# mLSTM heads with the bound on the squares and one f32 sum per token tile; a sixth output tile beside the last head

## The chip, the cores and the metric

The kernel runs on one core of one Trainium2 chip. The metric is the device time of one execution in microseconds (us), from three runs of the kernel before: 1195.31 us in the median, 1194.69 to 1196.02. A difference is told from no change here if it is over about 0.2%.

## The reference, cut to what matters

A trunk of two layers on 512 tokens of width 1024, all in float32. The first layer has four mLSTM heads of 192 columns beside four heads of attention to a memory; their outputs are joined to a mix of 1024 columns, multiplied by an output matrix and added to x. Then a gated MLP with a causal convolution follows; the second layer has band attention in place of the mLSTM. Of the mLSTM head, this counts here:

```python
num = einsum('bhts,bhse->bhte', s, vv) + inter[..., None] * einsum('bhtd,bhde->bhte', qq, c_st)
den = sum(s, axis=-1) + inter * einsum('bhtd,bhd->bht', qq, n_st)
h = num / maximum(abs(den), exp(-m_t))[..., None]
...
hm = hm * rsqrt(mean(hm * hm, axis=-1, keepdims=True) + EPS)      # per head, 192 columns
mix_out = hm * a_head_g * sigmoid(o)
...
x = x + concatenate([mix_out, mem_out], axis=-1) @ w_out
```

Since the division by the denominator and the norm are both factors per token, the kernel folds them into one: rsqrt(mean(num^2) + EPS * max(den^2, exp(-2 m_t))).

## The kernel before

Activations lie transposed: 128 features on the partitions, the 512 tokens (S) along the row; eight such tiles (KT) make up the width. A float32 product is made of three products of the faster fp32r type: both operands are split into a high part (cast, on ScalarE, L130) and a low part (difference, on VectorE, L131), and `mm3` (L167) issues high x high, high x low, low x high. Those three are called a triple here. A few small products stay in plain f32.

**A head (`mlstm_head`, L1144).** The whole sequence is worked as one causal square in four blocks of 128 tokens. `weighted_scores(s)` makes key-by-query scores in a "sc" bank of PSUM and weights them with spread exponents (L1155 to L1167); `products(s)` multiplies them by the values into two "tr" banks, `nums[0]` and `nums[1]`. A head has 192 columns: 128 in `nums[0]`, and 64 in one half of `nums[1]`. The value tiles carry 128 columns of ones between the heads' values, so that the other 64 rows of `nums[1]` all hold the denominator. Then come the squares of both banks on ScalarE (L1193), the product of the numerators and the output gate on VectorE (L1195), and per token tile two f32 products on TensorE (L1200, L1201) with the constant `mcf`: they give two columns per token, the sum of the numerators' squares and the denominator's square. Behind them are the maximum with `floor2` (L1205), two more small steps (L1206, L1207), an inverse square root in integer and float steps (`rsqrt`, L213), a diagonal matrix of the factor (`diagonal`, L231), its spread over the partitions by TensorE (`spread`, L244), the product with the gated numerators (L1214) and the split into the mix tiles (L1217). Heads 0 and 1 fill mix tiles 0 to 2, heads 2 and 3 tiles 3 to 5 (head 3: tile 5 and half of tile 4); the memory heads fill 6 and 7.

**The bound.** `gate_rows` (L1031) computes the gates' running sums as rows of 4 x 512 (head x token); `mr` (L1091, L1092) becomes m_t, at least -40. Four TensorE transposes (L1097) turn it into token columns, and one exponential (L1099) makes `floor2`.

**The order of the work.** Outside the blocks under `manual_schedule`, the order of the code is a wish: the framework orders each engine's instructions by its own estimate of when they are ready, with the code's order as priority; what is wrapped in `pin` keeps its place. Jobs are generators; `weave(job, filler, each)` (L200) advances the job, and for each of its yields (a bare one counts 1, `yield 2.673` counts 2.673) it takes `each` times so many steps of the filler, one step being a triple. In heads 0 to 2 the filler is the rest of the input projection (112 triples: tiles 2 to 5 and two tiles of memory queries). In the second memory attention and in head 3 it is the output projection.

**The output projection (`OutProjection`, L607).** Before, groups of output tiles accumulate early, in open banks: tiles 0 to 2 in the "mm" banks, 3 and 4 in the "tr" banks; `part(g, *ks)` loads and splits the weights of group g for the mix tiles ks and adds their products. `finish` (L627) takes the remaining output tiles (5, 6 and 7) as full projections, adds the residual (L633), and accumulates the squares of the next norm. The second layer uses the same class (L1380), with groups (0, 3) and (3, 5).

**Buffers.** Weights go through rings of three: "wr" as loaded, "wh" and "wl" the two parts. "u" has 57 tiles of 128x512, "t" eight. PSUM: three "mm" banks, three "sc", two "tr".

Of the kernel before, what the change touches and what calls it, by code (L numbers as in the profile page):

```python
# [9 lines left out]
F32 = mybir.dt.float32  # L10
# [3 lines left out]
ALU = mybir.AluOpType  # L14
# [41 lines left out]
def trunk(  # L56
# [30 lines left out]
    def sb(tag, shape, dtype=F32):  # L87
        count[0] += 1
        return pool.tile(shape, dtype, tag=tag, name=f"{tag}{count[0]}", bufs=bufs[tag])
# [23 lines left out]
    eps = cpool.tile([P, 1], F32, name="eps")  # L113
    V.memset(eps, EPS)

    mcf = cpool.tile([P, 3, 2], F32, name="mcf")
    V.memset(mcf, 0.0)
    V.memset(mcf[:, 0, 0:1], 1.0)
    V.memset(mcf[:HD, 1, 0:1], 1.0)
    V.memset(mcf[HD:, 1, 1:2], 1.0 / HD)  # L120
    V.memset(mcf[:HD, 2, 1:2], 1.0 / HD)
    V.memset(mcf[HD:, 2, 0:1], 1.0)


    HEADS = (slice(0, HD), slice(HD, P))

    pin = tc.keep_in_program_order
# [32 lines left out]
    def weights(*args):  # L160
        return parts(load(*args))

    def rows(w, c0, n, k0=0, k1=None):
        k1 = k1 if k1 is not None else w.shape[0] // P
        return w[k0 * P : k1 * P, c0 : c0 + n].rearrange("(k p) c -> p k c", p=P)
# [4 lines left out]
        nc.tensor.matmul(o, lh, rl, start=False, stop=False, skip_group_check=more)  # L170
        nc.tensor.matmul(o, ll, rh, start=False, stop=last, skip_group_check=more)  # L171

    def project(w, c0, act, tag="mm"):


        n = len(act)
        wh, wl = weights(rows(w, c0, P), n, P)
        o = ps(tag)
        for k in range(n):
            mm3(o, wh[:, k, :], wl[:, k, :], act[k][0], act[k][1], k == 0, k == n - 1)  # L180
            yield
        return o

    def run(gen):
        while True:
            try:
                next(gen)
            except StopIteration as end:
                return end.value

    def chain(*gens):
        for g in gens:
            yield from g
# [53 lines left out]
    def logarithms():  # L247

        pin(A.preload_act_table_set("natural_log_exp_and_others"))
# [357 lines left out]
    class OutProjection:  # L607
# [18 lines left out]

        def finish(self, gnames):  # L627
            logarithms()
            norm = Norm()
            acts = [[] for _ in gnames]  # L630
            for j in range(KT):
                o = self.o[j] if j in self.o else run(project(self.w, j * P, self.mixes))
                V.tensor_add(xT[j], xT[j], o)  # L633
                pin(G.dma_start(xspill[j], xT[j]))
                norm.add(xT[j])
                for a, g in zip(acts, gnames):
                    a.append(scaled(xT[j], g[:, j : j + 1]))
            return norm, acts
# [373 lines left out]
    e, u, c, r = (cpool.tile([P, TT, AH], F32, name=f"gate{i}") for i in range(4))  # L1012
    tot = cpool.tile([AH, 16], F32, name="tot")
    acol = cpool.tile([P, TT, AH], F32, name="acol")
    floor2 = cpool.tile([P, TT, AH], F32, name="floor2")
    NEXT = 4
    RO = [0, 512, 896, 1152, 1280]

# [12 lines left out]
    def gate_rows():  # L1031
# [58 lines left out]
            spread_exponents(i)  # L1090
        pin(V.tensor_tensor(out=mr, in0=mr, in1=br, op=ALU.add))  # L1091
        V.tensor_scalar(mr, mr, -40.0, None, op0=ALU.max)  # L1092
        yield
        tp = ps("tr")
        for T in range(TT):
            nc.tensor.transpose(tp[:, T * AH : (T + 1) * AH], ar[:, T * P : (T + 1) * P], ident[:AH, :AH])
            nc.tensor.transpose(tp[:, 16 + T * AH : 16 + (T + 1) * AH], mr[:, T * P : (T + 1) * P], ident[:AH, :AH])  # L1097
        pin(V.tensor_copy(acol, tp[:, :16].rearrange("p (t h) -> p t h", t=TT)))
        A.activation(floor2, tp[:, 16:32].rearrange("p (t h) -> p t h", t=TT), AF.Exp, scale=-2.0)  # L1099

    mixes = [None] * KT

# [41 lines left out]
    def mlstm_head(h):  # L1144
# [43 lines left out]
        yield from products(2)  # L1188
        yield from products(3)
        sqs = []  # L1190
        for o, j, r in ((nums[0], full, slice(0, P)), (nums[1], sh, rs)):
            sq = sb("t", [P, S])
            A.activation(sq, o, AF.Square)  # L1193
            sqs.append(sq)
            V.tensor_tensor(out=og[j][r, :], in0=o[r, :], in1=og[j][r, :], op=ALU.mult)  # L1195
        yield
        st = ps("sc")
        for T in range(TT):
            sl = slice(T * P, (T + 1) * P)
            nc.tensor.matmul(st[:, 2 * T : 2 * T + 2], sqs[0][:, sl], mcf[:, 0, :], start=True, stop=False)  # L1200
            nc.tensor.matmul(st[:, 2 * T : 2 * T + 2], sqs[1][:, sl], mcf[:, 1 + odd, :], start=False, stop=True)  # L1201
            yield 0.581
        st = st[:, : 2 * TT].rearrange("p (t c) -> p t c", c=2)
        z, fc = small(), small()
        V.tensor_tensor(out=z, in0=st[:, :, 1], in1=floor2[:, :, h], op=ALU.max)  # L1205
        V.tensor_scalar(z, z, EPS, 1e-35, op0=ALU.mult, op1=ALU.max)  # L1206
        V.scalar_tensor_tensor(z, st[:, :, 0], 1.0 / DH, z, op0=ALU.mult, op1=ALU.add)  # L1207
        rsqrt(fc, z)
        dg = diagonal(fc)
        yield 2.673  # L1210
        fb = spread(dg, "sc")
        yield
        for j, r in ((full, slice(0, P)), (sh, rs)):
# [2 lines left out]
                mixes[j] = sb("u", [P, S], F32R), sb("u", [P, S], F32R)  # L1216
            split(mixes[j][0][r, :], mixes[j][1][r, :], og[j][r, :])  # L1217

    outp = OutProjection(a_w_out, mixes, (0, 3, "mm"), (3, 5, "tr"))
    run(value_columns(1))  # L1220
    load_vectors(1)
    load_vectors(2)
# [16 lines left out]
    job = mlstm_head(3)  # L1239
    fill = chain(fill, outp.part(0, 7))  # L1240
    weave(islice(job, 13), fill, 0.85)
    fill = chain(fill, outp.part(1, 0, 1, 2, 6), outp.part(1, 3, 7))
    weave(job, fill, 0.862)
    run(chain(fill, outp.part(0, 4, 5), outp.part(1, 4, 5)))
    norm, (act,) = outp.finish([col["gffn"][:, 0:8]])


# [275 lines left out]
```

## Time and profile before

| What | Value |
|---|---|
| Median of three runs | 1195.31 us (1194.69 to 1196.02) |
| The profiled execution | 1195.72 us, span 1194.0 us |
| Granted TensorE clock | 0.999 of full speed |
| TensorE busy (PE) | 1183.5 us, 99% of the span |
| VectorE busy (DVE) | 961.7 us, 81% |
| ScalarE busy (ACT) | 725.2 us, 61% |
| GpSimd busy (POOL) | 130.3 us, 11% |
| Heads 0 to 3 with what is woven in | about 88 to 254 us of the span |

In the profile's lines, PE is TensorE's products, PEld its weight loads (beside PE), DVE VectorE, ACT ScalarE, POOL GpSimd, SP the queue that issues most DMAs. A line of a timeline gives start, length, engine, source line, operation, what it writes and reads (buffer numbers left out; psc, pmm and ptr are PSUM banks), its shape and how many like it were merged; in brackets stands the idle time before it and what ended that. The end of a TensorE product is modelled, so that lengths overlap; starts are measured.

### The profile page before, as it was taken

The page shows a single profiled execution, that of the slowest core. Times are in us where ns is not written, and L with a number is a line of the kernel's source. Part 1 is how long each engine was busy: PE and PEld are TensorE (multiplying, and loading weights), DVE is VectorE, ACT ScalarE, POOL GpSimd, SP SyncE. Part 2 cuts the span into 40 slices and gives each one's busy share as a digit, 9 for nine tenths or more (in the row PEclk, how much of TensorE's full clock was granted, in tenths as well). Part 3 has the DMA queues.
Part 4 walks back from the last instruction along what each step waited for, and adds up shares of the span by engine and source line. Part 5 has one row for each costly group of instructions (what it writes and reads, how often), then busy time and mean ns, then how long its engine had stood idle before and what let it go on. Part 6 is the DMA issues. An engine that isn't in the chain of part 4 may idle for free.

```text
span 1194.0 us, 18184 instructions
## 1 busy us (share of the span) xinstructions
PE 1183.5 (99%) x6719; PEld 1037.0 (87%) x6719; DVE 961.7 (81%) x1760; ACT 725.2 (61%) x1294; POOL 130.3 (11%) x222
## 2 busy tenths in 40 slices
PE   9999999999999999999999999999999999999997
PEld 9988888888899998999888888888889988999986
DVE  6877788788978888888698888997896888888855
ACT  5648677655656555555576677776565655555545
POOL 1211201010021111111020000101001011011100
PEclk9999999999999999999999999999999999999999
DMA  8645313444265676665464313246336455665551
GB/s 289 212 108 140 84 54 80 152 144 141 88 156 147 156 165 165 154 144 123 142 204 123 89 54 101 69 135 185 111 99 141 116 139 135 142 141 139 119 158 71
DMA packets 200155, 158.61 MB, mean 133 GB/s; under 512 B 8344, under 2 KB 179838, under 8 KB 200066
## 3 DMA queue, kind: packets, MB, share of 16 engines
q1 hardware_dynamic: 183906, 119.74, 34.1%
q0 software_dynamic: 15584, 36.67, 14.9%
q8 instruction: 53, 0.87, 0.3%
q10 hardware_dynamic: 576, 1.05, 0.2%
q14 instruction: 36, 0.29, 0.1%
HBM read 128.89 MB, written 32.46 MB: 135 GB/s over the span
## 4 chain that ended last, share of the span: by engine, by line
PE 92%; ACT 3%; DVE 2%; DMA 1%; SPq 1%; issue 0%; POOL 0%; POOLq 0%; DVEq 0%; ACTq 0%
PE pmm L169 15%; PE pmm L170 15%; PE pmm L171 15%; PE ptr L171 6%; PE ptr L169 6%; PE ptr L170 6%; PE pmm L785 6%; PE psc L171 5%; PE psc L170 5%; PE psc L169 5%; PE pmm L784 3%; PE psc L519 2%; PE ptr L1350 1%; DMA wr<-in_mem_w_kv_dram 1%; PE ptr L1371 1%; PE ptr L1372 1%
## 5 line engine op out<-in xcount | busy, mean ns | idle before, releaser
L169 PE MATMUL pmm<-u,wh 128*128 128x512 f32 (+1 forms) x872 | 309.1, 355 | 0.3 <-ACT u L130 0.2
L170 PE MATMUL pmm<-u,wh 128*128 128x512 f32 (+1 forms) x872 | 306.2, 351 | 0.0
L171 PE MATMUL pmm<-u,wl 128*128 128x512 f32 (+1 forms) x872 | 306.0, 351 | 0.0
L131 DVE TENSOR_TENSOR wl<-wr,wh 128x1024 fp32r<-128x1024 f32 (+3 forms) x172 | 199.8, 1163 | 57.0 <-ACT wh L130 55.0
L130 ACT CAST wh<-wr 128x1024 fp32r<-128x1024 f32 (+3 forms) x172 | 172.4, 1004 | 97.7 <-PE pmm L170 44.5
L171 PEld LDWEIGHTS pmm<-u,wl 128*128 128x128 f32 x872 | 164.5, 189 | 21.1
L169 PEld LDWEIGHTS pmm<-u,wh 128*128 128x128 f32 x872 | 164.5, 189 | 18.5 <-ACT u L130 1.1
L170 PEld LDWEIGHTS pmm<-u,wh 128*128 128x128 f32 x872 | 164.7, 189 | 18.2 <-DVE u L131 0.5
L169 PE MATMUL ptr<-u,wh 128*128 128x512 f32 x272 | 106.7, 392 | 0.0
L171 PE MATMUL ptr<-u,wl 128*128 128x512 f32 x272 | 106.1, 390 | 0.0
L753 POOL DMA_DIRECT2D xspill<-t x64 | 55.6, 869 | 461.1 <-ACT t L752 450.4
L170 PE MATMUL ptr<-u,wh 128*128 128x512 f32 x272 | 105.9, 389 | 0.0
L130 ACT CAST u<-pt 128x512 fp32r<-128x512 f32 x102 | 63.0, 620 | 46.8 <-DVE pt L875 46.7
L131 DVE TENSOR_TENSOR u<-pt,u 128x512 fp32r<-128x512 f32 x102 | 69.9, 688 | 11.2 <-ACT u L130 8.5
L169 PE MATMUL psc<-u,wh 128*128 128x256 f32 (+1 forms) x232 | 76.1, 328 | 0.0
L171 PE MATMUL psc<-u,wl 128*128 128x256 f32 (+1 forms) x232 | 75.9, 327 | 0.0
L170 PE MATMUL psc<-u,wh 128*128 128x256 f32 (+1 forms) x232 | 75.9, 327 | 0.0
L937 ACT ACTIVATE t<-t 128x512 f32<-128x512 f32 x34 | 21.6, 634 | 79.3 <-DVE t L660 79.3
L785 PE MATMUL pmm<-u,u 128*128 128x512 f32 x192 | 69.6, 397 | 0.0
L821 DVE TENSOR_TENSOR t<-t,pmm 128x256 f32<-128x256 f32 x72 | 30.2, 419 | 44.9 <-ACT t L819 44.8
L752 ACT COPY t<-ptr 128x512 f32<-128x512 f32 x64 | 37.4, 585 | 43.1 <-PE ptr L171 43.1
L660 DVE SCALAR_TENSOR_TENSOR t<-t,cols,t 128x511 f32<-128x511 f32 x80 | 59.7, 746 | 3.7 <-ACT t L667 3.7
(300 smaller groups left out, 2673.8 us busy)
## 6 DMA issues: line engine op xcount, KB each, us to landing
wr<-in_ffn_w_up_dram SPq DMA_DIRECT2D x54, 512.0 KB, 4.2
wr<-in_ffn_w_down_dram SPq DMA_DIRECT2D x38, 512.0 KB, 4.1
pt<-in_ffn_w_up_dram SPq DMA_DIRECT2D x34, 512.0 KB, 6.2
xspill<-t POOLq DMA_DIRECT2D x64, 256.0 KB, 5.2
wr<-in_a_w_in_dram SPq DMA_DIRECT2D x20, 512.0 KB, 3.7
xspill<-u POOLq DMA_DIRECT2D x32, 256.0 KB, 2.6
u<-xspill SPq DMA_DIRECT2D x32, 256.0 KB, 5.0
wr<-in_w_kv_dram SPq DMA_DIRECT2D x12, 512.0 KB, 3.7
```

Source lines behind the costliest of these rows:

```text
L130: high = A.copy(hi, src) if on_act else V.tensor_copy(hi, src)
L131: low = V.tensor_tensor(out=lo, in0=src, in1=f(hi), op=ALU.subtract)
L169: nc.tensor.matmul(o, lh, rh, start=first, stop=False, skip_group_check=more)
L170: nc.tensor.matmul(o, lh, rl, start=False, stop=False, skip_group_check=more)
L171: nc.tensor.matmul(o, ll, rh, start=False, stop=last, skip_group_check=more)
L519: nc.tensor.matmul(o, a, b, start=first and i == 0, stop=i == 1)
L660: V.scalar_tensor_tensor(acc[:, n:], src[:, : S - n], self.fw[:, c * FT + j : c * FT + j + 1], acc[:, n:], op0=ALU.mult, op1=ALU.add,)
L752: A.copy(t, o)
L753: G.dma_start(xspill[j], t, accum_op=ALU.add)
L784: nc.tensor.matmul(r[:, :H], w[1][:, k], p[i - 1][:, :H], start=False, stop=False, skip_group_check=True)
L785: nc.tensor.matmul(r, w[0][:, k], p[i - 1], start=False, stop=k == n - 1, skip_group_check=True)
L821: V.tensor_tensor(out=o, in0=o, in1=r[:, H:], op=ALU.add)
```

## The change

The bound is no longer turned into token columns. `mr` is made into max(EPS * 3 * exp(-2 m), 1e-35) as rows (DH / HD is 3, the factor between a sum over 64 equal rows and a mean over 192 columns), stored in DRAM, and loaded back as two "u" tiles in which the row of a head fills the 64 partitions where its denominator stands. In a head, the squares of `nums[1]` now come first; VectorE scales the denominator's half of them and takes the maximum with the bound, adds the two square tiles, and does the gate products after that. TensorE sums the added tile with a column of ones: one f32 product per token tile in place of two. After the sums one small step is left of three. The yields before the sums and before the spread change. In the output projection, tile 5 becomes a third group in a "sc" bank, its products beside the end of head 3, ahead of the group in the "tr" banks; `finish` loads and splits the weights of the first two remaining tiles before anything else, in both layers.

```diff
--- before.py
+++ after.py
@@ -113,15 +113,6 @@
     eps = cpool.tile([P, 1], F32, name="eps")
     V.memset(eps, EPS)
 
-    mcf = cpool.tile([P, 3, 2], F32, name="mcf")
-    V.memset(mcf, 0.0)
-    V.memset(mcf[:, 0, 0:1], 1.0)
-    V.memset(mcf[:HD, 1, 0:1], 1.0)
-    V.memset(mcf[HD:, 1, 1:2], 1.0 / HD)
-    V.memset(mcf[:HD, 2, 1:2], 1.0 / HD)
-    V.memset(mcf[HD:, 2, 0:1], 1.0)
-
-
     HEADS = (slice(0, HD), slice(HD, P))
 
     pin = tc.keep_in_program_order
@@ -170,11 +161,11 @@
         nc.tensor.matmul(o, lh, rl, start=False, stop=False, skip_group_check=more)
         nc.tensor.matmul(o, ll, rh, start=False, stop=last, skip_group_check=more)
 
-    def project(w, c0, act, tag="mm"):
+    def project(w, c0, act, tag="mm", ready=None):
 
 
         n = len(act)
-        wh, wl = weights(rows(w, c0, P), n, P)
+        wh, wl = ready or weights(rows(w, c0, P), n, P)
         o = ps(tag)
         for k in range(n):
             mm3(o, wh[:, k, :], wl[:, k, :], act[k][0], act[k][1], k == 0, k == n - 1)
@@ -626,10 +617,12 @@
 
         def finish(self, gnames):
             logarithms()
+            rest = [j for j in range(KT) if j not in self.o]
+            ready = {j: weights(rows(self.w, j * P, P), KT, P) for j in rest[:2]}
             norm = Norm()
             acts = [[] for _ in gnames]
             for j in range(KT):
-                o = self.o[j] if j in self.o else run(project(self.w, j * P, self.mixes))
+                o = self.o[j] if j in self.o else run(project(self.w, j * P, self.mixes, ready=ready.get(j)))
                 V.tensor_add(xT[j], xT[j], o)
                 pin(G.dma_start(xspill[j], xT[j]))
                 norm.add(xT[j])
@@ -1012,7 +1005,8 @@
     e, u, c, r = (cpool.tile([P, TT, AH], F32, name=f"gate{i}") for i in range(4))
     tot = cpool.tile([AH, 16], F32, name="tot")
     acol = cpool.tile([P, TT, AH], F32, name="acol")
-    floor2 = cpool.tile([P, TT, AH], F32, name="floor2")
+    floor2 = dram.tile([AH, S], F32, name="floor2")
+    floors = []
     NEXT = 4
     RO = [0, 512, 896, 1152, 1280]
 
@@ -1090,13 +1084,20 @@
             spread_exponents(i)
         pin(V.tensor_tensor(out=mr, in0=mr, in1=br, op=ALU.add))
         V.tensor_scalar(mr, mr, -40.0, None, op0=ALU.max)
+        A.activation(mr, mr, AF.Exp, scale=-2.0)
+        V.tensor_scalar(mr, mr, EPS * DH / HD, 1e-35, op0=ALU.mult, op1=ALU.max)
+        G.dma_start(floor2, mr)
+        for hp in range(2):
+            floors.append(sb("u", [P, S]))
+            for odd, half in enumerate(reversed(HEADS)):
+                row = floor2[2 * hp + odd]
+                src = bass.AP(tensor=row.tensor, offset=row.offset, ap=[[0, HD], [1, S]])
+                G.dma_start(floors[hp][half, :], src)
         yield
         tp = ps("tr")
         for T in range(TT):
             nc.tensor.transpose(tp[:, T * AH : (T + 1) * AH], ar[:, T * P : (T + 1) * P], ident[:AH, :AH])
-            nc.tensor.transpose(tp[:, 16 + T * AH : 16 + (T + 1) * AH], mr[:, T * P : (T + 1) * P], ident[:AH, :AH])
         pin(V.tensor_copy(acol, tp[:, :16].rearrange("p (t h) -> p t h", t=TT)))
-        A.activation(floor2, tp[:, 16:32].rearrange("p (t h) -> p t h", t=TT), AF.Exp, scale=-2.0)
 
     mixes = [None] * KT
 
@@ -1188,26 +1189,26 @@
         yield from products(2)
         yield from products(3)
         sqs = []
+        for o in reversed(nums):
+            sqs.insert(0, sb("t", [P, S]))
+            A.activation(sqs[0], o, AF.Square)
+        dr = HEADS[1 - odd]
+        V.scalar_tensor_tensor(
+            sqs[1][dr, :], sqs[1][dr, :], EPS * DH / HD, floors[hp][dr, :], op0=ALU.mult, op1=ALU.max
+        )
+        V.tensor_add(sqs[0], sqs[0], sqs[1])
         for o, j, r in ((nums[0], full, slice(0, P)), (nums[1], sh, rs)):
-            sq = sb("t", [P, S])
-            A.activation(sq, o, AF.Square)
-            sqs.append(sq)
             V.tensor_tensor(out=og[j][r, :], in0=o[r, :], in1=og[j][r, :], op=ALU.mult)
         yield
+        yield 3.6
         st = ps("sc")
         for T in range(TT):
-            sl = slice(T * P, (T + 1) * P)
-            nc.tensor.matmul(st[:, 2 * T : 2 * T + 2], sqs[0][:, sl], mcf[:, 0, :], start=True, stop=False)
-            nc.tensor.matmul(st[:, 2 * T : 2 * T + 2], sqs[1][:, sl], mcf[:, 1 + odd, :], start=False, stop=True)
-            yield 0.581
-        st = st[:, : 2 * TT].rearrange("p (t c) -> p t c", c=2)
+            nc.tensor.matmul(st[:, T : T + 1], sqs[0][:, T * P : (T + 1) * P], ones[:, :1], start=True, stop=True)
         z, fc = small(), small()
-        V.tensor_tensor(out=z, in0=st[:, :, 1], in1=floor2[:, :, h], op=ALU.max)
-        V.tensor_scalar(z, z, EPS, 1e-35, op0=ALU.mult, op1=ALU.max)
-        V.scalar_tensor_tensor(z, st[:, :, 0], 1.0 / DH, z, op0=ALU.mult, op1=ALU.add)
+        V.tensor_scalar(z, st[:, :TT], 1.0 / DH, None, op0=ALU.mult)
         rsqrt(fc, z)
         dg = diagonal(fc)
-        yield 2.673
+        yield 4.2
         fb = spread(dg, "sc")
         yield
         for j, r in ((full, slice(0, P)), (sh, rs)):
@@ -1216,7 +1217,7 @@
                 mixes[j] = sb("u", [P, S], F32R), sb("u", [P, S], F32R)
             split(mixes[j][0][r, :], mixes[j][1][r, :], og[j][r, :])
 
-    outp = OutProjection(a_w_out, mixes, (0, 3, "mm"), (3, 5, "tr"))
+    outp = OutProjection(a_w_out, mixes, (0, 3, "mm"), (3, 5, "tr"), (5, 6, "sc"))
     run(value_columns(1))
     load_vectors(1)
     load_vectors(2)
@@ -1239,9 +1240,9 @@
     job = mlstm_head(3)
     fill = chain(fill, outp.part(0, 7))
     weave(islice(job, 13), fill, 0.85)
-    fill = chain(fill, outp.part(1, 0, 1, 2, 6), outp.part(1, 3, 7))
+    fill = chain(fill, outp.part(2, 0, 1, 2, 3, 6, 7), outp.part(1, 0, 1, 2, 6), outp.part(1, 3, 7))
     weave(job, fill, 0.862)
-    run(chain(fill, outp.part(0, 4, 5), outp.part(1, 4, 5)))
+    run(chain(fill, outp.part(0, 4, 5), outp.part(1, 4, 5), outp.part(2, 4, 5)))
     norm, (act,) = outp.finish([col["gffn"][:, 0:8]])
```

## The prediction

> **What bounds the kernel now.** First the profile's page: its first section and the shares of the chain that ended last.
>
> ```profile
> PE 1183.5 (99%) x6719; PEld 1037.0 (87%) x6719; DVE 961.7 (81%) x1760; ACT 725.2 (61%) x1294; POOL 130.3 (11%) x222
> ...
> PE 92%; ACT 3%; DVE 2%; DMA 1%; SPq 1%; issue 0%; POOL 0%; POOLq 0%; DVEq 0%; ACTq 0%
> ```
>
> TensorE is busy for 99% of the span and is 92% of the chain: what shortens the run is a TensorE instruction less or a TensorE wait less, and work added on VectorE or ScalarE costs nothing until TensorE waits for it. Then the busy time of the stretch from the end of the gate rows to the end of head 3 (columns: length, then PE, PEld, DVE, ACT, POOL).
>
> ```profile
> core 0: us, PE busy (x) PEld busy (x) DVE busy (x) ACT busy (x) POOL busy (x), PEclk, DMA share, GB/s
> 88.00:254.00 166.00, 165.52 (x840) 138.89 (x839) 127.21 (x260) 114.80 (x193) 15.62 (x34) 1.00 0.39 102
> ```
>
> The stretch is like the whole: TensorE 165.52 of 166 us at full granted clock, VectorE 77%, ScalarE 69%. But a TensorE "busy" time is a modelled end; pace is read from start to start. So third, TensorE's timeline at head 3's sums.
>
> ```profile
> 241.49 0.28 PE L1200 MATMUL psc<-mcf,t 128*128 128x2 f32 x2
> 241.63 0.36 PE L1201 MATMUL psc<-mcf,t 128*128 128x2 f32 x2
> 241.85 0.36 PE L1200 MATMUL psc<-mcf,t 128*128 128x2 f32 x2
> 242.07 0.36 PE L1201 MATMUL psc<-mcf,t 128*128 128x2 f32 x2
> 242.30 0.49 PE L169 MATMUL ptr<-u,wh 128*128 128x512 f32 x1
> 242.62 0.40 PE L170 MATMUL ptr<-u,wh 128*128 128x512 f32 x1
> 242.85 0.40 PE L171 MATMUL ptr<-u,wl 128*128 128x512 f32 x1
> ```
>
> Ordinary 512-column products start 0.23 us apart (242.62 to 242.85); three of them, L169 to L171, are one triple, 0.69 us. Every f32 sum in the code stands as x2 in the trace, so one call is two passes. They have two columns each but a full 128x128 weight tile, and come about 0.11 us apart.
>
> **The change part by part.** *The f32 sums.* Eight passes and the product behind them take 242.62 − 241.49 = 1.13 us; less an ordinary 0.23 that is 0.90 us for eight passes, the slow restart of L169 (0.32) included. A head has four token tiles with two calls of two passes, 16 passes, two such blocks: 1.80 us. After the change it has four calls, eight passes: one block, 0.90. Lone calls would each pay the restart: the first two passes take 0.14 and the restart adds 0.09, 0.23 a call, 0.92 a head. A moving operand of one column instead of two changes nothing that I can see here, since the pace is far above two columns' share of 0.23. Saved: 0.9 us a head (0.88 to 0.9), 3.6 us for four heads, all of it on TensorE.
>
> The Trainium skill, page "TensorE: Matmul & The Clock Gate", section "Back-to-back issue gap", gives about 81 ns as the sustained spacing of a weight load and a small product; by it the 32 passes removed are worth 2.6 us. The 0.11 us of the rows is nearer to the weight load's own length by the same page, section "LDWEIGHTS" (columns / 1.2, so 107 ns), and I take the rows.
>
> *The transposes of the bound.* Four of L1097 go from the gate rows.
>
> ```profile
> 88.44 0.20 PE L1097 MATMUL ptr<-ident,t 4*128 4x4 f32 x1
> 88.50 0.20 PE L1096 MATMUL ptr<-ident,t 4*128 4x4 f32 x1
> ```
>
> They stand 0.06 us apart: 4 x 0.06 = 0.25 us saved.
>
> *The end of head 3.* Its rows 4 and 5 of the mix are the last thing that the output projection waits for.
>
> ```profile
> 251.75 0.39 PE L171 MATMUL ptr<-u,wl 128*128 128x512 f32 x1
> 252.30 0.96 PE L169 MATMUL pmm<-u,wh 128*128 128x512 f32 x3 [0.16 <-ACT u L130]
> 253.10 0.50 PE L170 MATMUL pmm<-u,wh 128*128 128x512 f32 x1
> 253.44 0.39 PE L171 MATMUL pmm<-u,wl 128*128 128x512 f32 x1
> ```
>
> From 251.75 to 253.44 five products start; at 0.23 that is 1.15 us, it took 1.69: 0.54 us are lost in waiting for the high and then the low part and in restarts. The chain behind it, on ScalarE and then on VectorE:
>
> ```profile
> 239.93 1.09 ACT L1193 ACTIVATE t<-ptr 128x512 f32<-128x512 f32 x2 [1.29 <-PE ptr L171]
> ```
> ```profile
> 240.56 0.69 DVE L1195 TENSOR_TENSOR u<-ptr,u 128x512 f32<-128x512 f32 x1 [1.20 <-ACT t L1193]
> ...
> 244.07 0.16 DVE L1205 TENSOR_TENSOR s<-psc,floor 128x4 f32<-128x4 f32 x1 [0.51 <-PE psc L1201]
> 244.27 0.17 DVE L1206 TENSOR_SCALAR s<-s 128x4 f32<-128x4 f32 x1
> ...
> 247.13 1.29 DVE L231 TENSOR_TENSOR t<-ident,s 128x512 fp32r<-128x512 f32 x2
> 249.23 1.42 DVE L1214 TENSOR_TENSOR u<-psc,u 128x512 f32<-128x512 f32 x2 [0.81 <-PE psc L244]
> 250.67 0.69 DVE L131 TENSOR_TENSOR wl<-wr,wh 128x512 fp32r<-128x512 f32 x1
> 251.63 1.41 DVE L131 TENSOR_TENSOR u<-u,u 128x512 fp32r<-128x512 f32 x2 [0.27 <-ACT u L130]
> ```
>
> Squares start at 239.93, the low parts are there at 251.63 + 1.41 = 253.04: 13.1 us. The change puts two VectorE instructions into this chain, the bound on 64 partitions and the addition. Their nearest rows:
>
> ```profile
> L501 DVE SCALAR_TENSOR_TENSOR u<-t,u x4: 673/685/689, 96.4 to 179.8; 64x512 fp32r<-64x512 f32 x4
> ```
> ```profile
> L264 DVE TENSOR_TENSOR rb<-rb,t x7: 684/689/691, 258.1 to 277.9; 128x512 f32<-128x512 f32 x7
> ```
>
> So + 0.69 + 0.69, of which the bound runs beside the second square; against that two small steps (L1205 to L1206, 0.20 apart) and half of the TensorE sums (0.9) go: between +0.1 and −0.6 us, and 0.7 more where VectorE has one more split like the one at 250.67 in front. Before that chain TensorE now has the sixth tile's six rows, 6 x 0.69 = 4.1 us of products that need neither a "tr" bank nor rows 4 and 5, less 0.9 of sums: 3.2 us more cover than before, where 0.54 was missing. The wait goes: −0.54. What is late next there is project 6, whose weights need the buffer of the row products (0; 4, 5): 4 + 2 triples (4.1 us) cover one cast and one subtraction. They are now issued ahead of the residual additions and squares, whose results nobody needs before the next norm. Total products of the projection are unchanged (8 x 8 triples); the split of one 1024-wide weight tile in two, and the early splits in the second layer, where projects 5 and 6 come behind the same rows, are laid at 0.
>
> *The bound as rows.* The gate rows get an exponential and a scaling of 4x512, a store and four broadcast loads on POOL's queue, in order.
>
> ```profile
> 83.81 0.52 DVE L1092 TENSOR_SCALAR t<-t 4x512 f32<-4x512 f32 x1
> ```
> ```profile
> 90.33 1.28 ACT L1099 ACT_TABLE_LOAD   x1
> ```
> ```profile
> 85.21 1.09 POOL L499 MEMSET u<- 64x512 f32 x2
> 100.53 0.55 POOL L1029 DMA_DIRECT2D bias<-exponents  x1 [14.22 <-ACT t L1155]
> ```
> ```profile
> exponents<-t POOLq DMA_DIRECT2D x1, 8.0 KB, 2.8
> ```
>
> If ScalarE takes the exponential at once (84.33, table load 1.28, about 0.55 as a square), then 0.52 on VectorE, 2.8 for the store to land, four issues of 0.55: 91.7. If it waits for the place of today's (90.33), 97.7. POOL is next needed at 100.53, for the exponents and the triangle of head 0, which are queued behind; even the late case leaves 2.8 us. Cost 0, and the two table loads at 90 and 93 us move rather than multiply. The bound itself is wanted at the end of head 0, over 20 us later. Its two "u" tiles and the longer hold of one "t" tile I lay at 0 as well. The removed memsets lie before the first input has landed: 0.
>
> *New waits.* The order moves: per head the pace units after the squares go from 6.0 to 8.8, so fill products are used up earlier. One such wait stands in the trace (timeline):
>
> ```profile
> 186.66 0.39 PE L169 MATMUL pmm<-u,wh 128*128 128x512 f32 x1
> 187.12 0.73 PE L519 MATMUL psc<-u,u 128*128 128x512 f32 x2
> 187.69 0.40 PE L170 MATMUL pmm<-u,wh 128*128 128x512 f32 x1
> ```
>
> Three starts from 186.66 to 187.69 took 1.03 for 0.69: 0.34 lost. New waits lie between −0.34 (this one vanishes) and some 3 us (rivals); I take one more of this size, +0.34.
>
> *Sum.* −3.6 − 0.25 − 0.54 + 0.34 = −4.05 us. The profiled execution took 1195.72 (span 1194.0 and 1.72 around it), 0.4 over the median 1195.31; I put the sum on the median: 1191.3.
>
> **The rivals.** *The sums wait for VectorE.* TensorE runs in order; the four sums now stand behind two VectorE steps. The 3.6 pace units before them are 5.0, 4.1, 5.1 and 3.1 triples in the four heads, so 2.1 us in head 3. Squares 1.09, then the addition 0.69: 1.8. Before, the sums started 0.47 us after the squares' end (241.02 to 241.49). If they keep that place, or one VectorE step of 0.69 stands in front of the addition, as L1195 did at 240.56, TensorE waits some 0.7 us; in all four heads 2.8 us: 1194.1. For it speaks VectorE's 77%; against it that the framework orders by estimated readiness, and that three heads have 0.7 us and more to spare. Chance 0.12.
>
> *Table switches.* In the chain of waits ScalarE runs back to back from 174 to 186 us, one switch in it:
>
> ```profile
> 175.90 1.28 ACT L1112
> ```
>
> The fill now runs some 7 triples ahead there, so other Silu and Exp work meets. Two switches more before the wait at 187 are 2.6 us: 1193.9. The Trainium skill, page "ScalarE: Activation LUTs", section "What ACT_TABLE_LOAD costs", puts a switch at 2.66 us with its drain; by it this rival is 1196.6. Against it: what moves away from there is a projection with four casts. Chance 0.06.
>
> *The small passes are cheaper than I read.* If they run at the pace of the first pair, 0.07 us a pass (241.49 to 241.63), and what I count beside it belongs to the products around them, eight passes are 0.56 and four heads save 2.2 us: 1192.7. The 81 ns quoted above from the Trainium skill's TensorE page would make it 1192.3. Against it: the second, third and fourth pair all keep 0.11. Chance 0.06.
>
> *Slower: head 2's end lies bare.* Fill before it counts 112 triples. By the paces heads 0 and 1, memory attention and head 2 used 107 and left 5; after the change they ask for all 112. If the planner has used them before the squares of head 2, its chain of 13.1 us has only the output projection's first rows to hide behind, and if those aren't split by then TensorE loses up to 10 us: 1201. It decides once more than 9 triples are missing. Against it:
>
> ```profile
> 209.40 0.83 ACT L130 CAST wh<-wr 128x768 fp32r<-128x768 f32 x1 [1.63 <-PE pmm L170]
> ```
>
> These first rows were split at 209.4, before head 2's factor had been spread. Chance 0.10.
>
> **How the numbers follow.** The forecast has 0.66. A measurement here tells about 0.2% (2.4 us) from no change: below 1192.9 is faster, above 1197.7 slower. Faster: 0.66 + 0.06 = 0.72; within: 0.12 + 0.06 = 0.18; slower 0.10. Low end: no new wait, the one at 187 gone too, and a half us of other restarts, 1195.31 − 3.6 − 0.25 − 0.54 − 0.34 − 0.5 = 1190.1. High end: the two cases within 0.2% lie at 1193.9 and 1194.1, with a small wait beside them 1194.5.
>
> **What would show it.** Right: f32 sums x32 in all instead of x64, about 0.9 us a head; no gap of TensorE before the rows 4 and 5; six triples in a "sc" bank right behind head 3's squares; span near 1190. Wrong: TensorE gaps in front of the sums with VectorE as releaser, more table loads between 160 and 190, a gap over 3 us near head 2's spread, or an unchanged span with fewer passes, which would mean that TensorE isn't what the heads wait for.

## The result, and the profile after

The change makes the kernel slower by a little: 1197.65 us (median of 14 runs, 1195.76 to 1199.99) against 1195.02 (14 runs, 1194.57 to 1196.02) on the same chip; ratio 1.0021, 95% interval 1.0013 to 1.0028. The profiled execution after took 1198.33 us with a span of 1196.6; before it was 1195.72 and 1194.0. The forecast was 1191.3, in a range of 1190.1 to 1194.5.

First the same views as before. The page's busy times and its chain, then the stretch of the heads. Lines have moved: a triple is now L160 to L162 (L169 to L171 before), the cast and the difference of a split L121 and L122 (L130, L131), a head's sums L1206, the spread L235 (L244).

```profile
PE 1183.4 (99%) x6683; PEld 1033.4 (86%) x6683; DVE 965.7 (81%) x1756; ACT 721.4 (60%) x1293; POOL 133.7 (11%) x227
...
PE 86%; DVE 5%; DMA 4%; ACT 3%; issue 1%; SPq 1%; POOL 0%; ACTq 0%; DVEq 0%; POOLq 0%
```

```profile
core 0: us, PE busy (x) PEld busy (x) DVE busy (x) ACT busy (x) POOL busy (x), PEclk, DMA share, GB/s
88.00:254.00 166.00, 162.86 (x798) 134.80 (x797) 130.53 (x258) 108.09 (x187) 20.01 (x40) 0.99 0.40 100
```

TensorE's part of the chain fell from 92 to 86%, and what came in its place is mostly VectorE and DMA. In the heads' 166 us TensorE is busy for 162.86, where it was busy for 165.52, and the granted clock is 0.99 instead of 1.00. The work removed is really gone; TensorE's timeline at head 0's sums and the groups of sums over the whole run (busy, mean ns, idle before):

```profile
131.72 0.95 PE L1206 MATMUL psc<-ones,t 128*128 128x1 f32 x8
132.53 0.49 PE L160 MATMUL pmm<-u,wh 128*128 128x512 f32 x1
132.85 0.40 PE L161 MATMUL pmm<-u,wh 128*128 128x512 f32 x1
```

```profile
L1206 PE MATMUL psc<-ones,t 128*128 128x1 f32 x32 | 3.8, 240 | 0.0
```

So the question is what was added. The waits view, TensorE from 88 to 285 us, after and then before:

```profile
PE ptr L160 <- ACT pt L121: 1.7, 1, 1.7
PE psc L510 <- DVE u L501: 0.5, 1, 0.5
PE psc L510 <- ACT t L567: 0.4, 1, 0.4
PE psc L235 <- DVE t L222: 0.4, 2, 0.2
```

```profile
PE pmm L169 <- ACT u L130: 0.2, 1, 0.2
PE ptr L169 <- ACT pt L130: 0.2, 1, 0.2
```

One wait stands out, in head 0. TensorE's timeline of after there:

```profile
121.51 0.39 PE L162 MATMUL pmm<-u,wl 128*128 128x512 f32 x1
123.62 0.33 PE L160 MATMUL ptr<-pt,u 128*128 128x128 f32 x1 [1.73 <-ACT pt L121]
...
125.44 0.63 PE L160 MATMUL pmm<-u,wh 128*128 128x512 f32 x1
125.87 0.63 PE L161 MATMUL pmm<-u,wh 128*128 128x512 f32 x1
```

Start to start, 123.62 − 121.51 = 2.11 us passed where 0.23 would do: 1.88 lost. Then the ordinary products come 0.43 us apart instead of 0.23. The stretches in three equal windows show why (the last three columns: granted clock, DMA share, GB/s):

```profile
121.74:125.15 3.41, 1.68 (x10) 1.29 (x10) 0.98 (x2) 2.73 (x5) 0.00 (x0) 1.00 0.20 64
125.15:128.56 3.41, 3.41 (x10) 2.63 (x9) 3.14 (x5) 2.30 (x4) 0.00 (x0) 0.50 0.02 5
128.56:131.97 3.41, 3.41 (x19) 2.82 (x17) 1.89 (x3) 0.00 (x0) 0.00 (x0) 1.00 0.26 61
```

For 3.41 us the granted clock is a half, so 3.41 / 2 = 1.7 us more are lost. What TensorE waits for is the cast of head 0's last score block, 128x128, on ScalarE. ScalarE's timeline of after:

```profile
94.47 1.05 ACT L121 CAST wh<-wr 128x1024 fp32r<-128x1024 f32 x1 [3.12 <-DMA wr<-in_a_w_in_dram]
...
109.68 1.99 ACT L121 CAST wh<-wr 128x1024 fp32r<-128x1024 f32 x2
...
112.54 0.52 ACT L121 CAST pt<-t 128x384 fp32r<-128x384 f32 x1 [0.36 <-DVE t L1167]
116.52 1.05 ACT L121 CAST wh<-wr 128x1024 fp32r<-128x1024 f32 x1 [3.46 <-DMA wr<-in_a_w_in_dram]
117.47 0.40 ACT L121 CAST pt<-t 128x256 fp32r<-128x256 f32 x1
...
123.29 0.28 ACT L121 CAST pt<-t 128x128 fp32r<-128x128 f32 x1
```

and the pieces of the chain that ended last which lead there (start, length, what):

```profile
110.32 6.12 DMA wr<-in_a_w_in_dram
...
116.52 1.06 ACT wh L121
...
117.60 1.23 DVE wl L122
...
121.46 1.28 ACT L1113
...
123.38 0.20 ACT pt L121
```

In before the order on ScalarE is another one:

```profile
102.08 1.04 ACT L130 CAST wh<-wr 128x1024 fp32r<-128x1024 f32 x1
...
112.79 0.41 ACT L130 CAST pt<-t 128x256 fp32r<-128x256 f32 x1 [0.33 <-DVE t L1166]
...
114.12 1.06 ACT L130 CAST wh<-wr 128x1024 fp32r<-128x1024 f32 x1
...
119.84 0.28 ACT L130 CAST pt<-t 128x128 fp32r<-128x128 f32 x1
```

After, a weight cast stands at 94.47 that stood at 102.08; another stands in front of the 128x256 score block instead of behind it, and holds ScalarE for 3.46 us until its load, issued at 110.32, has landed. Everything queued behind it comes late. The way to the last score block leads over VectorE: the difference of the late weight tile (L122), a query tile's convolution (L1112), that tile's activation on ScalarE with its table load (L1113), and then the block's cast, at 123.29 instead of 119.84. The load took 6.12 us; the one issued at 110.21 in before was used at 114.12, so it took 3.9 at most.

A ledger from the gate rows' first transpose (88.35 before, 88.20 after) to the first product of the projection's norm (280.43, 281.86): 192.08 us before, 193.66 after, so +1.58. The forecast took 4.39 away there (sums, transposes, head 3's end). New: 1.88 for this wait, 1.7 for the half clock, 0.70 at 105 us (head 0's scores, L510, behind L501), 0.35 at each of two spreads (L235, at 138.91 and 216.88), 0.57 at 177 us (L510 behind L567), 0.26 at 188, and about 0.5 in slow restarts (some 0.1 us more to the next start behind a wait): 6.3; about 0.4 of old waits (at 187 and 233) are gone. That makes +1.5. Behind the norm another +1.15 us came, two waits in the channel mixer near 321 and 327 us (0.32 and 0.66 us start to start), both for the low part of a weight tile. The two stretches hold the same products but for the 36 passes that the change removes (954 and 918 in the traces). Ledgers here and below are read from one profiled execution of each kernel, which lies up to 1.4 us from the median of its runs.

### The profile page after: what moved, and what is told of

It is laid out like the page before. It is cut to its first block, busy times and chain, and to the rows that moved or that the text cites. A ratio compares the mean times of both kernels' runs of the same rounds, so it can differ in the third digit from the quotient of the medians.

```text
span 1196.6 us, 18129 instructions
## 1 busy us (share of the span) xinstructions
PE 1183.4 (99%) x6683; PEld 1033.4 (86%) x6683; DVE 965.7 (81%) x1756; ACT 721.4 (60%) x1293; POOL 133.7 (11%) x227
## 4 chain that ended last, share of the span: by engine, by line
PE 86%; DVE 5%; DMA 4%; ACT 3%; issue 1%; SPq 1%; POOL 0%; ACTq 0%; DVEq 0%; POOLq 0%
PE pmm L160 13%; PE pmm L161 13%; PE pmm L162 13%; PE ptr L161 6%; PE ptr L162 6%; PE ptr L160 6%; PE pmm L778 6%; PE psc L162 5%; PE psc L160 5%; PE psc L161 5%; PE pmm L777 3%; PE psc L510 2%; DMA wr<-in_a_w_in_dram 2%; PE ptr L1351 1%; DVE wl L122 1%; DMA pt<-in_x_dram 1%
## 5 line engine op out<-in xcount | busy, mean ns | idle before, releaser
L160 PE MATMUL pmm<-u,wh 128*128 128x512 f32 (+1 forms) x864 | 306.1, 355 | 0.1
L162 PE MATMUL pmm<-u,wl 128*128 128x512 f32 (+1 forms) x864 | 303.8, 352 | 0.2 <-DVE wl L122 0.2
L122 DVE TENSOR_TENSOR wl<-wr,wh 128x1024 fp32r<-128x1024 f32 (+5 forms) x173 | 199.9, 1156 | 64.8 <-ACT wh L121 63.0
L121 ACT CAST wh<-wr 128x1024 fp32r<-128x1024 f32 (+5 forms) x173 | 172.1, 997 | 111.5 <-PE pmm L161 52.0
L162 PEld LDWEIGHTS pmm<-u,wl 128*128 128x128 f32 x864 | 163.3, 189 | 21.5 <-DVE wl L122 0.6
L160 PEld LDWEIGHTS pmm<-u,wh 128*128 128x128 f32 x864 | 163.4, 189 | 18.3 <-ACT u L121 0.5
L160 PE MATMUL ptr<-u,wh 128*128 128x512 f32 x272 | 106.5, 392 | 0.0
L162 PE MATMUL ptr<-u,wl 128*128 128x512 f32 x272 | 106.1, 390 | 0.0
L121 ACT CAST u<-pt 128x512 fp32r<-128x512 f32 x102 | 62.8, 618 | 46.7 <-DVE pt L868 46.6
L162 PE MATMUL psc<-u,wl 128*128 128x256 f32 (+1 forms) x240 | 79.2, 330 | 0.5 <-DVE wl L122 0.5
L160 PE MATMUL psc<-u,wh 128*128 128x256 f32 (+1 forms) x240 | 79.3, 331 | 0.0
L122 DVE TENSOR_TENSOR u<-pt,u 128x512 fp32r<-128x512 f32 x102 | 70.1, 689 | 11.2 <-ACT u L121 8.5
L161 PE MATMUL psc<-u,wh 128*128 128x256 f32 (+1 forms) x240 | 79.0, 329 | 0.0
```

Source lines behind the costliest of these rows:

```text
L121: high = A.copy(hi, src) if on_act else V.tensor_copy(hi, src)
L122: low = V.tensor_tensor(out=lo, in0=src, in1=f(hi), op=ALU.subtract)
L160: nc.tensor.matmul(o, lh, rh, start=first, stop=False, skip_group_check=more)
```

## The experiments

The theory (A): the change's head part reorders ScalarE's queue around head 0, so that a weight cast that waits for a load stands ahead of a score block's cast. Rivals: (B) the projection part (sixth tile, early splits) costs the time; (C) the new pace (3.6 and 4.2 units) uses up fill; (D) the loads are late whatever the order. Each time is the median of 11 runs unless said, each ratio is to the kernel before on the same chip, with its 95% interval.

**The heads alone.** The changed kernel with the old projection:

```
-            ready = {j: weights(...) for j in rest[:2]}
+            ready = {}
...
-    outp = OutProjection(a_w_out, mixes, (0, 3, "mm"), (3, 5, "tr"), (5, 6, "sc"))
+    outp = OutProjection(a_w_out, mixes, (0, 3, "mm"), (3, 5, "tr"))
...
```

> The changed kernel with the output projection as before (two groups, three late projects, no early split). Theory A (the loss is made in the heads: a late weight load in head 0 holds ScalarE's queue, TensorE waits some 2 us and then runs at half clock): as slow as the changed kernel or slower by the 0.5 us that head 3's end costs again, 1197 to 1199. Rival B (the loss comes from the sixth tile and the early splits, and the heads bring the 4 us forecast): 1191 to 1192.

Measured: 1197.98 us, ratio 1.0018 (1.0009 to 1.0027). The wait of head 0 (1.8 us at 121.0) and the half clock behind it are there, the waits in the channel mixer are not. B falls: the heads alone make the whole loss.

**The projection alone.** The kernel before with the sixth tile and the early splits:

```
+            ready = {j: weights(rows(self.w, j * P, P), KT, P) for j in rest[:2]}
...
-    outp = OutProjection(a_w_out, mixes, (0, 3, "mm"), (3, 5, "tr"))
+    outp = OutProjection(a_w_out, mixes, (0, 3, "mm"), (3, 5, "tr"), (5, 6, "sc"))
...
```

> The kernel before with the sixth tile in a sc bank and the early splits, heads untouched. Theory A: 1194.5 to 1195.0, at most the 0.5 us of head 3's end gained. Rival B: 1198 or more.

Measured: 1196.59 us, ratio 1.0004 (0.9995 to 1.0013). Head 3's end wait is gone, a wait of 0.2 us at 326 us is new. The median lies between the two ranges, and the interval doesn't tell it from the kernel before: the 0.54 us of head 3's end aren't seen in the time.

**The old pace.** The changed kernel with the paces of before around the sums (2.324 is four times 0.581; those four yields stood between the sums, here they stand together ahead of them):

```
-        yield 3.6
+        yield 2.324
...
-        yield 4.2
+        yield 2.673
```

> The changed kernel with the yields before the sums and the spread as they were (2.324 in place of 3.6, 2.673 in place of 4.2), so that the fill is used at the old rate. Theory A as stated does not hang on the pace: 1197 to 1199, the head 0 wait still there, since the pace acts only behind head 0's squares. Rival C (the new pace uses the fill up too early and causes the waits in heads 1 to 3, some 2 us): 1195 to 1196.

Measured (5 runs): 1202.17 us, ratio 1.0051 (1.0038 to 1.0064). The wait of 1.8 us in head 0 stays, so it doesn't come from the pace; new waits of 0.76, 0.23 and 1.0 us stand at 185 to 188 us, with a half clock behind them. The time is above both ranges. C falls: the new pace is the faster one, by some 4 us.

**Memory keys later.** In the changed kernel the load and the split of memory attention's keys and values are issued behind head 0:

```
-    memkv = load_memory_kv(0)
     weave(mlstm_head(0), fill, 1.4)
+    memkv = load_memory_kv(0)
```

> The changed kernel with the load and split of the memory's keys and values issued behind head 0 instead of ahead of it. Before head 0 it holds one of the three buffers of raw weights until 110 us, and two 512 KB loads then run at once. Theory A: with the buffer free the weights land in time, head 0's wait (2.3 us) and the half clock (1.7 us) go: 1193 to 1195. Rival D (ScalarE's queue is late in head 0 for another reason, such as the additional exponential and its table): 1197 to 1199, the wait before head 0's last products stays.

Measured: 1193.37 us, ratio 0.9984 (0.9975 to 0.9993). ScalarE's timeline now has the two score blocks ahead of the weight cast, which waits for nothing:

```profile
112.49 0.41 ACT L121 CAST pt<-t 128x256 fp32r<-128x256 f32 x1 [0.96 <-DVE t L1167]
112.80 1.04 ACT L121 CAST wh<-wr 128x1024 fp32r<-128x1024 f32 x1
...
119.24 0.28 ACT L121 CAST pt<-t 128x128 fp32r<-128x128 f32 x1
```

The wait and the half clock are gone, and the stretch of the ledger (87.88 to 277.28) takes 189.40 us, 2.68 less than before. D falls as it was put: with the loads and casts in another order the gain is there. This run moves both, so it doesn't say which of them counts. The weight cast that after had moved to 94.47 is early here too (93.08), so an early cast alone does no harm. What still lies between that and the 4.39 forecast for the stretch are 0.35 us at each of two spreads, 0.57 at 173 us and slow restarts; a wait of 0.6 us at 322 comes behind the norm. No version that was run has a lower median.

**The same move on the kernel before.** Is that gain the move's own?

> The kernel before, with the load and split of memory attention's keys and values issued behind head 0 instead of ahead of it; nothing of the change is in it. Theory: the wait that this order makes in head 0 belongs to the changed heads (before had no wait there), so here little moves: 1194.2 to 1195.3, and the same move on the changed kernel, which gave 1193.37, has the change worth 1 to 2 us. Rival: this order holds up the weight casts in any kernel, and what the run of the changed kernel with the later load gained on the kernel before is the move's gain and not the change's: 1192.5 to 1193.5 here.

Measured: 1195.91 us, ratio 1.0001 (0.9992 to 1.0009), 0.6 above the theory's range and far from the rival's. The move by itself gains nothing. So with the casts in a harmless order the change is worth about 2 us (0.8 to 3.0 by the interval of the run above).

**Later memory keys, heads alone** (the two edits above together):

> The changed heads with the later memory keys, and the old output projection (five tiles beside the heads, no early splits). Theory: the TensorE wait of 0.6 us near 322 us in the channel mixer comes from the projection part and goes here, head 3's end wait of 0.8 us comes back: the same time as with the new projection, 1193.0 to 1193.9. Rival: the new projection is worth its 0.54 us and the wait at 322 is not its doing: 1193.8 to 1194.5, with the wait near 322 still there. Other rival: the new projection costs more than it brings: below 1192.9.

Measured: 1194.12 us, ratio 0.9984 (0.9975 to 0.9993). The time is 0.2 above the theory's range, but its waits are the theory's: none near 322, and head 3's end lost 0.84 us at 239 and 0.27 at 246. The new projection takes 1.5 us less up to the norm (189.40 against 190.87) and gives 0.8 back in the channel mixer; the medians, 0.75 apart, are from different chips and can't tell more.

**Sixth tile without the early splits.** The version with the later memory keys, and

```
-            ready = {j: weights(rows(self.w, j * P, P), KT, P) for j in rest[:2]}
+            ready = {}
```

> The changed kernel with the later memory keys and the sixth tile beside head 3, but without the early splits of the last two weight tiles. Theory: the early splits shift the weight ring by two tiles and so make the wait near 322 us; without them it is gone, head 3's end wait stays gone: 1192.4 to 1193.1. Rival: the sixth tile itself makes that wait, or the early splits hide as much: 1193.2 to 1194.

Measured (6 runs): 1199.96 us, ratio 1.0037 (1.0024 to 1.0049). Both theories missed. TensorE's timeline, and windows behind it:

```profile
262.41 0.39 PE L161 MATMUL pmm<-u,wh 128*128 128x512 f32 x1
265.80 0.80 PE L160 MATMUL pmm<-u,wh 128*128 128x512 f32 x1 [3.00 <-ACT wh L121]
266.39 0.63 PE L161 MATMUL pmm<-u,wh 128*128 128x512 f32 x1
```

```profile
265.80:269.20 3.40, 3.03 (x6) 1.99 (x7) 3.40 (x5) 0.57 (x1) 0.00 (x0) 0.50 0.13 31
269.20:272.60 3.40, 3.40 (x10) 2.62 (x9) 1.06 (x1) 0.00 (x0) 0.00 (x0) 0.53 0.84 238
```

Without the early splits project 6's cast stands on ScalarE behind the norm's squares, TensorE waits 3.2 us, and the clock is halved for 6.8 us, 3.4 more. The early splits aren't an extra: without them the sixth tile costs about 6.5 us here (1199.96 against 1193.37, on two chips).

**One early split.** The same version, and

```
-            ready = {j: weights(rows(self.w, j * P, P), KT, P) for j in rest[:2]}
+            ready = {j: weights(rows(self.w, j * P, P), KT, P) for j in rest[:1]}
```

> The changed kernel with the later memory keys and one early split of the projection's last weight tiles instead of two. Without any, TensorE waited 3.4 us at 262 us and the clock was halved behind it; with both it waits 0.6 us at 322 us. Theory: the first of the two is the one that the projection needs, the second moves the weight ring into the channel mixer: no wait at 262 and none at 322, 1192.4 to 1193.2. Rival: the second is needed too, a wait of some us comes at 265 to 270: 1195 to 1199.

Measured: 1194.18 us, ratio 0.9989 (0.9980 to 0.9997), between the two ranges. Each had a part right: a wait of 1.27 us moves to project 7, with no half clock behind it, and the channel mixer's waits are gone.

```profile
267.81 0.39 PE L161 MATMUL pmm<-u,wh 128*128 128x512 f32 x1
269.31 0.50 PE L162 MATMUL pmm<-u,wl 128*128 128x512 f32 x1 [1.10 <-DVE wl L122]
```

**The rows path alone.** The kernel before with the bound's exponential, scaling, store and four loads added, their result unused:

```
+        er = sb("t", [P, S])[:AH, :]
+        A.activation(er, mr, AF.Exp, scale=-2.0)
+        V.tensor_scalar(er, er, EPS * DH / HD, 1e-35, op0=ALU.mult, op1=ALU.max)
+        G.dma_start(floorrow, er)
...
+                G.dma_start(floors[hp][half, :], src)
```

> The kernel before with the bound's row path added and its result unused: an exponential and a scaling of 4x512 in the gate rows, the store and the four broadcast loads on POOL's queue, two u buffers held; sums, paces and projection as before. Theory: this path, which I had laid at 0, puts off the weight loads around the memory keys, and a good part of the wait of 2 us in head 0 near 121 us appears: 1196.2 to 1197.8. Rival: the path costs nothing and the order of the heads alone moves the casts: 1194.9 to 1195.6, no wait of TensorE over 1 us between 118 and 126 us.

Measured: 1195.26 us, ratio 0.9996 (0.9987 to 1.0005), no wait of TensorE over 1 us near 121. The new path costs nothing, as forecast. Then what moved the casts? Pace, projection and the added rows are out; left are what the change takes away in the gate rows, and the heads' new end.

**The old exponential kept.** The changed kernel with four transposes and the late exponential of 128x16 put back, on other data, into a tile that nobody reads:

```
+            nc.tensor.transpose(tp[:, 16 + T * AH : ...], ar[:, T * P : ...], ident[:AH, :AH])
...
+        A.activation(spare, tp[:, 16:32].rearrange(...), AF.Exp, scale=-2.0)
```

> The changed kernel with the four transposes and the late exponential of 128x16 of the gate rows put back, on other data and into a tile that nobody reads; nothing else. Theory: that exponential with its two table switches held a place of some 2.8 us in ScalarE's order; with it gone one weight cast was put ahead, the loads behind it moved round their ring of three, and the cast in head 0 came to stand behind a late load. With it back ScalarE's order around head 0 is again that of before: no TensorE wait over 1 us near 121 us, no half clock behind it, the wait at 105 us gone too, 1192.5 to 1194.2, although it adds work. Rival: the order follows from the heads' new end (squares, sums), and the wait of 2 us in head 0 stays: 1197.4 to 1198.4.

Measured: 1194.36 us, ratio 0.9989 (0.9980 to 0.9998). ScalarE's timeline:

```profile
91.18 0.18 ACT L1103 ACTIVATE spare<-ptr 128x16 f32<-128x16 f32 x1
91.26 1.04 ACT L121 CAST wh<-wr 128x1024 fp32r<-128x1024 f32 x1
...
101.25 1.03 ACT L121 CAST wh<-wr 128x1024 fp32r<-128x1024 f32 x1
...
112.56 0.41 ACT L121 CAST pt<-t 128x256 fp32r<-128x256 f32 x1 [0.96 <-DVE t L1170]
...
114.37 1.06 ACT L121 CAST wh<-wr 128x1024 fp32r<-128x1024 f32 x1 [0.43 <-DMA wr<-in_a_w_in_dram]
```

The cast is back at 101.25, and the one at 114.37 stands behind the 128x256 block as it did before; the wait and the half clock are gone, the wait at 105 us too, and the ledger's stretch (87.68 to 276.89) takes 189.21 us: 4.45 less than the changed kernel's, with more work in it. The median is 0.16 above the theory's range and far from the rival's. So what put the weight cast ahead was a step taken away: the small exponential of 0.18 us with its table load, and the four transposes that feed it, which this run puts back together.

**One cast on VectorE.** The changed kernel, its order as it is, with head 0's last score block cast by VectorE:

```
-            split(pt[...], pt[...], e[:, :n])
+            split(pt[...], pt[...], e[:, :n], on_act=(h, s) != (0, 3))
```

> The changed kernel with one cast of head 0 (the high part of its last score block, 128x128) taken from ScalarE to VectorE; the weight cast ahead of it on ScalarE still waits 3.5 us for its load. Theory: TensorE waits for this cast alone, because of its place in ScalarE's queue; VectorE has the block weighted at 121.6, so the wait falls from 2.1 to about 0.4 us, and the half clock that follows it (1.7 us) doesn't come: 1194 to 1195.3. Rival: TensorE waits for the load itself or for the scores, and the wait stays over 1.5 us: 1197 to 1198.4. In between: the wait falls and the half clock comes all the same: 1195.6 to 1196.4.

Measured: 1194.81 us, ratio 0.9995 (0.9987 to 1.0004). ScalarE, VectorE and TensorE:

```profile
115.70 1.05 ACT L121 CAST wh<-wr 128x1024 fp32r<-128x1024 f32 x1 [3.50 <-DMA wr<-in_a_w_in_dram]
```
```profile
120.48 0.28 DVE L1167 SCALAR_TENSOR_TENSOR t<-psc,t 128x128 f32<-128x128 f32 x1
120.80 0.23 DVE L121 CAST pt<-t 128x128 fp32r<-128x128 f32 x1
```
```profile
120.64 0.39 PE L162 MATMUL pmm<-u,wl 128*128 128x512 f32 x1
121.08 0.33 PE L160 MATMUL ptr<-pt,u 128*128 128x128 f32 x1
```

ScalarE waits for the load as long as in the changed kernel, but TensorE only 0.44 − 0.23 = 0.21 us, and no half clock follows. The ledger's stretch is 190.32 us, 3.34 less than the changed kernel's: 1.88 − 0.21 of wait and 1.7 of half clock are 3.4. TensorE waited neither for that load's weights nor for the scores, but for a cast of 0.28 us in its place in ScalarE's queue.

**More pace.** The version with the later memory keys, with more pace ahead of the spread:

```
-        yield 4.2
+        yield 5.0
```

> The version with the later memory keys (1193.37 before), and 5.0 instead of 4.2 pace units between the sums and the spread of a head's factor, so that 0.8 x 1.4 triples more stand in front of the spread. Theory: the 0.35 us that TensorE waits there in heads 0 and 2 (133.4, 211.8) are a matter of pace and go with some 0.2 us of restarts: 1192.3 to 1193.1. Rival: the later order brings new waits (ScalarE's order changes from head 0's end on, with two table loads more), as the first change of order did: 1193.5 to 1196.

Measured: 1195.69 us, ratio 1.0004 (0.9995 to 1.0013). That is in the rival's range. The wait of head 0's spread (133) stays, the one of head 2's goes, and new ones come: 0.75 us start to start in front of head 1's sums at 154, which wait for VectorE (L1199), 0.3 at head 1's spread, and about 0.6 each at 187 and 196.

## Why the prediction was wrong

- *The f32 sums, −3.6*: right. By the working of the prediction head 0's block costs 132.85 − 131.72 − 0.23 = 0.90 us, the other three 0.90 to 0.93, and there is one a head. The rival of cheaper passes falls.
- *The transposes, −0.25, and head 3's end, −0.54*: right; they are gone and so is the gap. That project 6 is late next and needs its weights issued early is borne out: without the early splits about 6.5 us are lost. What they do further on stood at nothing without a reason: with two of them weights come late in the channel mixer, where about 1 us came back, and with one or none they don't. Taken alone the projection part measures as nothing.
- *The bound as rows, 0*: right for the path that is added (the run with the rows alone). The store took 4.9 us instead of 2.8, and POOL came to its memsets at 95.4, still ahead of its next need. Wrong for what the same edit takes away, and here the step failed: "Cost 0, and the two table loads at 90 and 93 us move rather than multiply". They did move, to 84 and 87, and didn't multiply; what had no reason was the 0 for the place that they and the small exponential left on ScalarE. A weight cast took it, 7.6 us earlier than before (94.47, before 102.08). With it moved the ring of three load buffers, the casts behind it, and the score block's cast. I had costed that place as one on an idle engine; it was a place in an order that a scheduler makes. Its price was 1.88 us of wait and 1.7 of half clock in head 0, and the 0.70 at 105 us, which are gone too with the step put back. Putting the step back gives 0.9989 instead of 1.0021.
- *New waits, +0.34 with a bound of 3*: this term of the sum was mis-sized; it is about 5.9 us up to the norm (6.3 new, 0.4 gone) and 1.15 behind it. More than half of the 5.9 is head 0's wait and its half clock. No rival had this wait, and none had the half clock, which nearly doubled its price.
- *The rivals.* TensorE's sums show 0.0 idle before them; ScalarE loads 2 tables between 160 and 190 us where before it loaded 5; head 2's spread waits 0.35 us, not the 3 or more of the slower case. That case had the right sign by luck: the gap that its mechanism would leave there isn't in the trace.
- *What stays open*: why the load issued at 110.32 took 6.12 us when one issued at 110.21 before took 3.9 at most. With 3.9 the weight cast would have waited 1.2 us and not 3.46. From 111 to 113 us the DMA engines moved 70 GB/s at a busy share of 0.63, where before they moved 237 at 0.91. The traces show one difference. GpSimd issued a broadcast of exponents (bias) at 110.07, 0.25 us ahead of this load; before, at 110.45, it was 0.24 behind it. It is 0.24 ahead in all three other runs with ScalarE's wait of over 3 us, too (heads alone, old pace, cast on VectorE), and behind the load by 0.07 to 0.21 in the projection alone, the rows alone and the old exponential kept, where the cast starts 4.3 to 4.8 us after the issue. No run swaps these two issues alone, so that their order makes the load late isn't shown; nor has any run the late load with the casts in the old order, or the reverse.

## What to carry to other kernels

When a step is taken off an engine that isn't the bound, ask what will slide into its place, which buffer or load that takes, and which short instruction then stands behind it in that engine's queue. Where a scheduler sets the order, a gain of work and a loss of order are priced separately: compare the queues of the two kernels instruction by instruction before costing an edit at nothing. And look at the order near any gap of TensorE of about 2 us: head 0's cost nearly twice its length here.

## What the runs showed of the hardware

The half clock came in stretches of 3.41 us or twice that, each following a stretch of 3.41 us in which TensorE had little work. Ahead of the halving it was busy for 1.68 of 3.41 us in the changed kernel, and for 1.77 with the heads alone. With the old pace two stretches have little work, head 0's and the one at 185 us:

```profile
120.12:123.53 3.41, 2.01 (x12) 1.41 (x10) 1.59 (x3) 1.89 (x3) 0.06 (x1) 1.00 0.63 171
123.53:126.94 3.41, 3.15 (x16) 2.64 (x17) 2.33 (x5) 2.74 (x7) 0.00 (x0) 1.00 0.00 0
184.97:188.38 3.41, 1.96 (x10) 1.15 (x10) 2.41 (x6) 3.40 (x7) 0.00 (x0) 1.00 0.04 15
188.38:191.79 3.41, 3.41 (x9) 2.60 (x8) 2.79 (x5) 1.96 (x4) 0.37 (x1) 0.50 0.00 0
```

The limits are laid back from the start of the half clock at 188.38, in steps of the length that the trace records for it (188.385 to 191.798, 3.413 us); that the stretches follow each other without a break is taken for granted there. The same 1.8 us of wait in head 0 falls here across two stretches (2.01 and 3.15 busy), and nothing is halved; three short waits in one stretch (1.96 busy) are followed by it. The Trainium skill, page "TensorE: Matmul & The Clock Gate", section "Part 1: The HAM clock gate", has a free-running window of about 3.4 us and the half clock after at least one idle window. The length agrees; "idle" doesn't: a window with TensorE busy for a half was enough. Where the bound lies, between 1.96 and 2.01 by these modelled busy times, is a guess from a few cases.
